# Evictions and pair combinations of the seven-product half-steps placed by scheduler priority

## The chip, the cores and the metric

One core of one Trainium2 chip runs the whole program. TensorE (PE in the rows; its weight loads are listed apart as PEld) multiplies, VectorE (DVE) and ScalarE (ACT) do arithmetic on tiles, GpSimd (POOL) and SyncE (SP) mainly issue transfers here. The metric is device time in microseconds for one execution, the median of several runs.

## The reference

The kernel is one inference step of a two-layer decoder: 512 tokens of a prompt and 8 sample tokens, 520 columns together, share all weights. Each layer is a half-step, a mixer (attention with a gated linear recurrence in layer 0, a matrix-memory recurrence in layer 1) and a second half-step. Only the four half-steps are touched by the change:

```python
D_MODEL = 1024; D_FF = 2816

def swiglu(x, w_gate, w_up, w_down):
    return (jax.nn.silu(x @ w_gate) * (x @ w_up)) @ w_down

def macaron_half(x, g, w_gate, w_up, w_down):
    return x + (0.5 * swiglu(rmsnorm(x, g), w_gate, w_up, w_down)).astype(x.dtype)

for li in range(DEPTH):          # DEPTH = 2
    x = macaron_half(x, g[0], ...)
    x = x + mixer(li, rmsnorm(x, g[1]))
    x = macaron_half(x, g[2], ...)
```

All arithmetic is in f32.

## The kernel before

**Numbers.** PE multiplies operands that are split into a high and a low part (`split`, L110 to L112: ACT casts the high part, `whi` for weights, then DVE subtracts it to make the low part, `wlo`). `dense` (L94 to L108) issues three matmuls for each 128x128 block: high by high, high by low, low by high (L106, L107, L108).

**A half-step** (`half_step`, called four times by `ffn`, at about 0, 785, 1145 and 1836 us of the span) goes over the 22 blocks of 128 hidden columns in groups of 6, 6, 6 and 4. The first four blocks, the lead gates, are plain products (`early`, tiles `g` and `u`); they run while the normalised input is still being made ready. After them come units: a `Gate` unit makes the hidden tile `h` of one block for all columns, a `Down` unit adds one pair of 128-row blocks to `x`. After every group but the last, eight `Down` units for that group stand between the first gate of the next group and the rest of them.

**A unit** is a two-by-two block product made with seven products instead of eight, named p1, q5, q6, p2, p3, p7 and p4 (`WHERE` tells which weights and which operand each takes). A product is 12 matmuls in a Gate unit or a Down unit of four blocks, 9 in a Down unit of three. Its three accumulators are PSUM banks: `A` takes p1, q6, p7 and p4, `B` takes p2, `E` takes q5 and p3. The products add up in a bank, which is why a bank is read between two products:

- after p1, ACT copies A to B (`evict`, L655);
- Gate: q5 is copied to `c5` by ACT (the rows' c<-E, L655), q6 to `h` by ACT, p2 goes through Silu on ACT (L519), p3 is added on DVE (L521) and goes through Silu on ACT, p7 is added to `c5` on DVE (c<-A, L524) and multiplied into `h` (L525), p4 is multiplied into `h` on DVE (L528);
- Down: each product is added to `x` on DVE (x<-A, x<-E, x<-B, L552).

The six banks go round in one pool. The loop over the units (`for f in seq`) issues, for each, `weights(f)`, p1 and q5, then p4 of the unit before, then q6, p2, p3 and p7. A matmul that goes on in a bank has to wait until that bank's last product was read.

**Weights.** `weights(f)` loads `graw` and `u2` on SP's queue, `raw` partly on SP's and, with an add on the way, on POOL's; then it makes five operands from them with three casts on ACT, three subtractions and two adds on DVE, and one more cast and subtraction for the sums. There are five buffers for full-size parts, two for `graw`; the pair tile of the lead gates shares one of the `graw` buffers.

**Pairs.** Two neighbouring Gate units fill one pair tile `h`. When both are done, `Pair.combine` makes the seven operands of the Down units: DVE instructions `cmb` (L468, L471, L472), casts `hh` on ACT and subtractions `hl` on DVE. It was called at the end of the odd gate's p4 and, for the lead pairs, once after the first unit's q5.

**What sets the order.** A scheduler places the instructions of all engines. Among those that could run it takes the one with the earliest place in the program; `tc.high_priority(n)` counts what is issued in its block as n places earlier. Weights' parts of a unit stand under `AHF` = 200. Evictions and combinations stood at their own place.

Of the kernel before, what the change touches and what calls it, by code (L numbers as in the profile page):

```python
# [35 lines left out]
REST = 4  # L36

AHM, AHF, AHE = 1, 200, 100
WHL = 5
SLOPE = [2.0 ** (-2 * (h + 1)) for h in range(4)]  # L40

# [20 lines left out]
class Net:  # L62
# [186 lines left out]
    def ffn(self, steps):  # L249
# [3 lines left out]
        with ExitStack() as ctx:  # L253
            self.wgrp = UNIT
            xp = self.pool(ctx, "ffnx")
            self.whl = self.pool(ctx, "whl", WHL)
            hp = self.pool(ctx, "ffn")
# [7 lines left out]
    def half_step(self, pos, first, last, xp, hp, pa):  # L265
# [9 lines left out]
        nc, tc = self.nc, self.tc  # L275
# [108 lines left out]
        def step():  # L384
            if steps and next(steps[0], 0) == 0:
                steps.pop(0)
# [54 lines left out]
        def bank(name):  # L441
            return pa.tile([P, 512], F32, tag="acc", name=name)

        def small():
            return hp.tile([P, n1], F32, tag="c5", name="c5")

        class Pair:
# [15 lines left out]
                self_split(hidden[0][:, self.i, j:j + b - a], hidden[1][:, self.i, j:j + b - a], self.h[:, a:b])  # L463

            def combine(self):
                x11, x22, x21, x12 = [self.h[:, i] for i in range(4)]
                cm = hp.tile([P, 4 * n1], F32, tag="cmb", name="cmb").rearrange("p (s t) -> p s t", s=4)
                nc.vector.tensor_tensor(out=cm[:, 0:2], in0=self.h[:, 0:2], op=ALU.subtract,  # L468
                                        in1=x12[:, None, :].to_broadcast([P, 2, n1]))
                self.parts(0, 3, 0)  # L470
                nc.vector.scalar_tensor_tensor(cm[:, 2], cm[:, 1], -1.0, x11, ALU.mult, ALU.subtract)  # L471
                nc.vector.scalar_tensor_tensor(cm[:, 3], cm[:, 2], -1.0, x21, ALU.mult, ALU.subtract)  # L472
                for a in (0, 2):
                    self_split(hidden[0][:, self.i, 3 + a:5 + a], hidden[1][:, self.i, 3 + a:5 + a], cm[:, a:a + 2])
# [6 lines left out]
        class Unit:  # L481

            def product(f, kind):
                w, v = WHERE[kind]
                n = n0 if kind in ("p1", "p2", "p4") else n1
                if kind == "p1":
                    f.A, f.B = bank("A"), bank("B")
                elif kind == "q5":
                    f.E = bank("E")
                ps = f.B if kind == "p2" else f.E if kind in ("q5", "p3") else f.A  # L490
                self.dense(ps[:, :n], f.w[w], lambda k: tuple(q[:, :n] for q in f.rhs(v, k)), ends=(kind in ("p1", "q5"), True),
                           open_=True)
                if kind == "p1":
                    self.evict(f.B[:, :n0], ps[:, :n0])
                f.out(kind, ps[:, :n])
                step()

        class Gate(Unit):
            nk = H
# [10 lines left out]
            def out(f, kind, ps):  # L510
                if kind in ("q6", "p2"):
                    f.pair.open()
                if kind == "q5":
                    f.c5 = small()
                    self.evict(f.c5, ps)
                elif kind == "q6":
                    self.evict(f.h(1), ps)
                elif kind == "p2":
                    nc.scalar.activation(f.h(0), ps, AF.Silu)  # L519
                elif kind == "p3":  # L520
                    nc.vector.tensor_tensor(out=f.h(1), in0=ps, in1=f.h(1), op=ALU.add)  # L521
                    nc.scalar.activation(f.h(1), f.h(1), AF.Silu)
                elif kind == "p7":
                    nc.vector.tensor_tensor(out=f.c5, in0=ps, in1=f.c5, op=ALU.add)  # L524
                    nc.vector.tensor_tensor(out=f.h(1), in0=f.h(1), in1=f.c5, op=ALU.mult)  # L525
                    f.done(1)
                elif kind == "p4":
                    nc.vector.tensor_tensor(out=f.h(0), in0=ps, in1=f.h(0), op=ALU.mult)  # L528
                    f.done(0)
                    if f.odd and not f.pair.plain:  # L530
                        f.pair.combine()

            def done(f, c):
                if f.pair.plain and not f.late:
# [1399 lines left out]
```

## Time and profile before

| | us |
|---|---|
| median of 3 runs | 2192.76 |
| lowest, highest run | 2188.43, 2197.22 |
| the profiled execution: time | 2194.01 |
| the profiled execution: span from the first to the last instruction | 2192.2 |
| PE busy in the span | 2130.5 |
| DVE busy | 1629.2 |
| ACT busy | 1108.1 |
| mean granted clock of PE (full speed is 1) | 0.992 |

The 1.8 us between time and span lie before the first and after the last instruction. Each row of a timeline is a start, a duration and, in brackets, the idle time of the engine before it with what ended it. Matmuls are pipelined: each lasts about 0.28 us, but the next starts 0.12 us later, so lost time on PE shows in the distance of starts.

### The profile page before, as it was taken

How to read it: one execution, taken by the hardware profiler on the slowest of the kernel's cores; microseconds unless marked ns; L12 is line 12 of the kernel's file. 1: busy time of each engine (PE TensorE's matmuls, PEld its weight loads, DVE VectorE, ACT ScalarE, POOL GpSimd, SP SyncE). 2: the span in 40 equal slices, each digit the busy share in tenths (PEclk: the TensorE clock that was granted, in tenths of full speed). 3: DMA queues.
4: the chain of work that ended last, by engine and by line, in shares of the span. 5: the costliest groups of instructions: out<-in, count | busy, mean ns of one | idle time of the engine just before them, and what ended most of it. 6: DMA issues, size and time to landing. Idle time of an engine off the chain costs nothing.

```text
span 2192.2 us, 46399 instructions
## 1 busy us (share of the span) xinstructions
PE 2130.5 (97%) x17908; PEld 2001.1 (91%) x17908; DVE 1629.2 (74%) x3409; ACT 1108.1 (51%) x2080; POOL 194.6 (9%) x276
## 2 busy tenths in 40 slices
PE   8999999999999999999999999999999999999999
PEld 8899999776776799999999999998989899999999
DVE  8888887434486587888877888877745588788884
ACT  6555555334523354556554565654555456455653
POOL 1011101000000001111100111100000000111110
PEclk9999999999999999999999999999999999999999
DMA  7487764478787745867733677653554564676872
GB/s 214 118 207 169 180 169 144 155 261 264 233 264 249 240 143 128 209 159 191 186 126 84 167 179 193 161 147 94 149 158 147 167 195 152 139 204 166 191 182 73
DMA packets 175763, 381.29 MB, mean 174 GB/s; under 512 B 16353, under 2 KB 51730, under 8 KB 175414
## 3 DMA queue, kind: packets, MB, share of 16 engines
q1 hardware_dynamic: 129600, 283.23, 39.6%
q0 software_dynamic: 40176, 82.05, 20.9%
q10 hardware_dynamic: 5766, 13.05, 1.6%
q8 instruction: 140, 2.29, 0.4%
q14 instruction: 81, 0.66, 0.1%
HBM read 361.15 MB, written 17.11 MB: 173 GB/s over the span
## 4 chain that ended last, share of the span: by engine, by line
PE 74%; DVE 13%; DMA 9%; ACT 3%; issue 2%; SPq 0%; ACTq 0%; DVEq 0%; POOLq 0%
PE A L106 9%; PE A L108 8%; PE A L107 8%; PE E L106 4%; PE E L107 4%; PE E L108 4%; DVE wlo L112 4%; PE pj L106 4%; PE pj L108 3%; PE pj L107 3%; PE y L106 2%; DMA raw<-w 2%; PE y L107 2%; PE y L108 2%; PE B L108 2%; PE B L107 2%
## 5 line engine op out<-in xcount | busy, mean ns | idle before, releaser
L112 DVE TENSOR_TENSOR wlo<-raw,whi 128x512 fp32r<-128x512 f32 (+2 forms) x344 | 311.9, 910 | 106.1 <-ACT whi L111 101.6
L111 ACT CAST whi<-raw 128x512 fp32r<-128x512 f32 (+2 forms) x344 | 273.2, 799 | 153.8 <-PE pj L107 76.6
L112 DVE TENSOR_TENSOR wlo<-graw,whi 128x1024 fp32r<-128x1024 f32 (+1 forms) x240 | 266.4, 1115 | 113.3 <-ACT whi L111 112.2
L111 ACT CAST whi<-graw 128x1024 fp32r<-128x1024 f32 (+1 forms) x240 | 231.2, 965 | 154.4 <-PE B L107 90.0
L106 PE MATMUL pj<-xh,whi 128*128 128x264 f32 (+1 forms) x896 | 258.8, 291 | 4.3 <-ACT kT L655 1.5
L106 PE MATMUL A<-xb,whi 128*128 128x264 f32 (+1 forms) x864 | 250.8, 290 | 8.2 <-DVE c L524 4.7
L108 PE MATMUL pj<-xh,wlo 128*128 128x264 f32 (+1 forms) x896 | 254.3, 285 | 1.5 <-DVE wlo L112 1.5
L107 PE MATMUL pj<-xl,whi 128*128 128x264 f32 (+1 forms) x896 | 255.0, 285 | 0.8 <-DVE xl L112 0.7
L107 PE MATMUL A<-xb,whi 128*128 128x264 f32 (+1 forms) x864 | 244.7, 283 | 0.6 <-DVE xb L112 0.6
L108 PE MATMUL A<-xb,wlo 128*128 128x264 f32 (+1 forms) x864 | 245.0, 284 | 0.0
L429 POOL DMA_DIRECT2D raw<-w x120 | 142.1, 1184 | 1141.3 <-DMA raw<-w 402.7
L106 PEld LDWEIGHTS pj<-xh,whi 128*128 128x128 f32 x896 | 169.1, 189 | 20.5 <-issue 9.5
L106 PEld LDWEIGHTS A<-xb,whi 128*128 128x128 f32 x864 | 163.4, 189 | 13.4 <-DVE c L524 5.9
L107 PEld LDWEIGHTS pj<-xl,whi 128*128 128x128 f32 x896 | 169.6, 189 | 5.1 <-DVE xl L112 2.5
L108 PEld LDWEIGHTS pj<-xh,wlo 128*128 128x128 f32 x896 | 169.6, 189 | 4.5 <-issue 2.7
L106 PE MATMUL A<-hh,whi 128*128 128x264 f32 (+1 forms) x576 | 165.5, 287 | 2.0
L106 PE MATMUL E<-xh,whi 128*128 128x264 f32 x576 | 163.6, 284 | 3.9 <-ACT c L655 3.9
L107 PEld LDWEIGHTS A<-xb,whi 128*128 128x128 f32 x864 | 163.1, 189 | 0.8 <-DVE xb L112 0.8
L107 PE MATMUL E<-xl,whi 128*128 128x264 f32 x576 | 163.4, 284 | 0.0
L108 PEld LDWEIGHTS A<-xb,wlo 128*128 128x128 f32 x864 | 163.3, 189 | 0.0
L108 PE MATMUL E<-xh,wlo 128*128 128x264 f32 x576 | 163.2, 283 | 0.0
L107 PE MATMUL A<-hl,whi 128*128 128x264 f32 (+1 forms) x576 | 162.7, 282 | 0.0
(491 smaller groups left out, 6266.9 us busy)
## 6 DMA issues: line engine op xcount, KB each, us to landing
raw<-w SPq DMA_DIRECT2D x168, 512.0 KB, 4.2
raw<-w POOLq DMA_DIRECT2D x112, 512.0 KB, 6.9
graw<-w SPq DMA_DIRECT2D x72, 512.0 KB, 4.2
kt<-ckt SPq DMA_DIRECT2D x128, 256.0 KB, 4.4
vtile<-cv SPq DMA_DIRECT2D x128, 256.0 KB, 4.0
u<-w SPq DMA_DIRECT2D x72, 256.0 KB, 3.7
raw<-w SPq DMA_DIRECT2D x48, 384.0 KB, 3.7
raw<-w POOLq DMA_DIRECT2D x48, 384.0 KB, 5.6
```

The source lines that it names most:

```text
L106: nc.tensor.matmul(ps, lhsT=wh, rhs=xh, start=(ends[0] and i == ks[0]), stop=False, skip_group_check=open_)
L107: nc.tensor.matmul(ps, lhsT=wh, rhs=xl, start=False, stop=False, skip_group_check=open_)
L108: nc.tensor.matmul(ps, lhsT=wl, rhs=xh, start=False, stop=(ends[1] and i == ks[-1]), skip_group_check=open_)
L111: self.nc.scalar.copy(out=hi, in_=src)
L112: self.nc.vector.tensor_tensor(out=lo, in0=src, in1=hi, op=ALU.subtract)
L429: nc.gpsimd.dma_start(out=s2, in_=w[f.u0:f.u0 + 2, :, :B].rearrange("u p c -> p u c"), accum_op=ALU.add)
```

## The change

A product's `out` (the evictions after q5, q6, p2, p3, p7 and p4, and what is computed from them) is issued under a priority of 300 places, so ahead of the weights' parts of a later unit, which stand at 200. The copy of A to B after p1 stays as it was. A pair's combination is issued under a priority of 100 places, in a new method `after` that is called once `out` is done; the lead pairs' combination takes the same path. Nothing is added to or removed from any engine's instructions.

```diff
 AHM, AHF, AHE = 1, 200, 100
+AHO, AHC = 300, 100
 
             def combine(self):
+                with tc.high_priority(AHC):
+                    self.combined()
+
+            def combined(self):
                 x11, x22, x21, x12 = [self.h[:, i] for i in range(4)]
...
                 if kind == "p1":
                     self.evict(f.B[:, :n0], ps[:, :n0])
-                f.out(kind, ps[:, :n])
+                with tc.high_priority(AHO):
+                    f.out(kind, ps[:, :n])
+                f.after(kind)
                 step()
+
+            def after(f, kind):
+                pass
...
                     f.done(0)
-                    if f.odd and not f.pair.plain:
-                        f.pair.combine()
+
+            def after(f, kind):
+                if kind == "p4" and f.odd and not f.pair.plain:
+                    f.pair.combine()
```

Lines move by one near the top of the file and by ten to twelve lower down: L106 becomes L107, L112 becomes L113, L524 becomes L534, L552 becomes L564, L655 becomes L667.

DVE at the first hand-over from Down units to the next Gate unit (first half-step). A_2550 and A_2648 are the A banks of the last two Down units of the group, E_2660 the last one's E; 2721 to 2733 are the weights of the Gate unit behind them. Before:

```order
L552 SCALAR_TENSOR_TENSOR x_69<-E_2562,x_69 128x264
L112 TENSOR_TENSOR wlo_2729<-graw_2721,whi_2728 128x1024
L112 TENSOR_TENSOR wlo_2737<-raw_2725,whi_2736 128x1024
L432 TENSOR_TENSOR graw_2721<-graw_2721,raw_2725 128x512
L552 SCALAR_TENSOR_TENSOR x_69<-A_2550,x_69 128x264
L432 TENSOR_TENSOR graw_2721<-graw_2721 128x512
L552 SCALAR_TENSOR_TENSOR x_69<-E_2660,x_69 128x264
L552 SCALAR_TENSOR_TENSOR x_69<-A_2648,x_69 128x264
L552 SCALAR_TENSOR_TENSOR x_69<-A_2550,x_69 128x256
L112 TENSOR_TENSOR wlo_2733<-u2_2723,whi_2732 128x512
```

After:

```order
L564 SCALAR_TENSOR_TENSOR x_69<-E_2562,x_69 128x264
L113 TENSOR_TENSOR wlo_2729<-graw_2721,whi_2728 128x1024
L564 SCALAR_TENSOR_TENSOR x_69<-A_2550,x_69 128x264
L113 TENSOR_TENSOR wlo_2737<-raw_2725,whi_2736 128x1024
L564 SCALAR_TENSOR_TENSOR x_69<-E_2660,x_69 128x264
L433 TENSOR_TENSOR graw_2721<-graw_2721,raw_2725 128x512
L564 SCALAR_TENSOR_TENSOR x_69<-A_2550,x_69 128x256
L113 TENSOR_TENSOR wlo_2733<-u2_2723,whi_2732 128x512
L564 SCALAR_TENSOR_TENSOR x_69<-A_2648,x_69 128x264
L433 TENSOR_TENSOR graw_2721<-graw_2721 128x512
```

The evictions of the two Down units now stand between the parts of the next unit's weights: the one of A_2550 behind one subtraction, where it stood behind two and an add.

ACT at the start of the second half-step. A_13094, B_13095 and E_13109 are the banks of the second Gate unit there, 13191 to 13195 the weights of the third. Before:

```order
L655 ACTIVATE B_13095<-A_13094 128x256
L111 CAST whi_13198<-graw_13191 128x1024
L111 CAST whi_13206<-raw_13195 128x1024
L111 CAST whi_13202<-u2_13193 128x512
L655 ACTIVATE c5_13122<-E_13109 128x264
L655 ACTIVATE h_13025<-A_13094 128x264
L519 ACTIVATE h_13025<-B_13095 128x256
```

After:

```order
L667 ACTIVATE B_13095<-A_13094 128x256
L112 CAST whi_13198<-graw_13191 128x1024
L667 ACTIVATE c5_13122<-E_13109 128x264
L112 CAST whi_13206<-raw_13195 128x1024
L112 CAST whi_13202<-u2_13193 128x512
L667 ACTIVATE h_13025<-A_13094 128x264
L529 ACTIVATE h_13025<-B_13095 128x256
```

The copy of E to c5 stood behind three casts of the next unit's weights and now stands behind the first.

DVE at the same place, some 7 us on; A_13094 again, 13325 to 13329 are the weights of the fourth unit. Before:

```order
L112 TENSOR_TENSOR wlo_13213<-graw_13191,whi_13212 128x1024
L112 TENSOR_TENSOR wlo_13333<-graw_13325,whi_13332 128x768
L112 TENSOR_TENSOR wlo_13341<-raw_13329,whi_13340 128x768
L432 TENSOR_TENSOR graw_13325<-graw_13325,raw_13329 128x384
L524 TENSOR_TENSOR c5_13122<-A_13094,c5_13122 128x264
L432 TENSOR_TENSOR graw_13325<-graw_13325 128x384
```

After:

```order
L113 TENSOR_TENSOR wlo_13213<-graw_13191,whi_13212 128x1024
L534 TENSOR_TENSOR c5_13122<-A_13094,c5_13122 128x264
L113 TENSOR_TENSOR wlo_13333<-graw_13325,whi_13332 128x768
L535 TENSOR_TENSOR h_13025<-h_13025,c5_13122 128x264
L113 TENSOR_TENSOR wlo_13341<-raw_13329,whi_13340 128x768
L433 TENSOR_TENSOR graw_13325<-graw_13325,raw_13329 128x384
```

The eviction c5<-A_13094 (of p7) moved up over two subtractions and an add.

PE at the same start. A_12955 is the A bank of the first Gate unit, whose p4 is due. Before:

```order
L106 MATMUL A_13094<-xh_70,whi_13076 128x256
L107 MATMUL A_13094<-xl_71,whi_13076 128x256
L108 MATMUL A_13094<-xh_70,wlo_13077 128x256
L106 MATMUL E_13109<-xh_70,whi_13084 128x264
L107 MATMUL E_13109<-xl_71,whi_13084 128x264
L108 MATMUL E_13109<-xh_70,wlo_13085 128x264
```

After:

```order
L107 MATMUL A_13094<-xh_70,whi_13076 128x256
L108 MATMUL A_13094<-xl_71,whi_13076 128x256
L109 MATMUL A_13094<-xh_70,wlo_13077 128x256
L107 MATMUL A_12955<-xb_12394,whi_12941 128x256
L107 MATMUL E_13109<-xh_70,whi_13084 128x264
L108 MATMUL E_13109<-xl_71,whi_13084 128x264
```

The first matmul of the first unit's p4 now stands between p1 and q5 of the second; its other eleven stand behind q5 as before. One unit on, the first matmul of A_13094's p4 moved in the same way.

At the start of the first half-step the three cmb instructions of the first lead pair moved up DVE's order by some 13 to 15 places, to between the lead gates' own evictions (h<-g).

## Rows read from the trace of the kernel before

**Rows 1.** The page's first part: busy us, share of the span, instructions.

```profile
PE 2130.5 (97%) x17908; PEld 2001.1 (91%) x17908; DVE 1629.2 (74%) x3409; ACT 1108.1 (51%) x2080; POOL 194.6 (9%) x276
```

**Rows 2.** Waits of PE by releaser: us in total, times, longest.

```profile
PE A L106 <- DVE c L524: 4.7, 5, 1.4
PE E L106 <- ACT c L655: 3.9, 4, 1.1
```

**Rows 3.** The same view of the weight loads.

```profile
PEld A L106 <- DVE x L552: 7.1, 24, 0.4
```

**Rows 4.** Stretches: length, busy us (instructions) by engine, granted clock, DMA share, GB/s.

```profile
160.00:200.00 40.00, 40.00 (x333) 39.79 (x331) 34.33 (x60) 22.62 (x39) 4.96 (x6) 1.00 0.69 152
840.00:880.00 40.00, 37.70 (x308) 36.99 (x307) 33.38 (x53) 22.11 (x38) 3.75 (x5) 1.00 0.59 134
```

**Rows 5.** Timeline of PE, first hand-over: start, us, line, operation, idle before.

```profile
214.47 0.28 PE L108 MATMUL A<-hh,wlo 128*128 128x264 f32 x1
214.78 0.39 PE L106 MATMUL A<-hh,whi 128*128 128x256 f32 x1
```

**Rows 6.** Timeline of DVE, the same hand-over.

```profile
211.42 1.23 DVE L112 TENSOR_TENSOR wlo<-graw,whi 128x1024 fp32r<-128x1024 f32 x1
212.56 1.22 DVE L112 TENSOR_TENSOR wlo<-raw,whi 128x1024 fp32r<-128x1024 f32 x1
...
214.30 0.42 DVE L552 SCALAR_TENSOR_TENSOR x<-A,x 128x264 f32<-128x264 f32 x1
```

**Rows 7.** Timeline of PE, start of the second half-step.

```profile
852.30 0.28 PE L106 MATMUL E<-xh,whi 128*128 128x264 f32 x1
...
858.24 0.28 PE L108 MATMUL B<-xh,wlo 128*128 128x256 f32 x1
859.43 0.39 PE L106 MATMUL E<-xh,whi 128*128 128x264 f32 x1 [0.91 <-ACT c L655]
...
863.86 0.28 PE L106 MATMUL E<-xh,whi 128*128 128x264 f32 x1
...
867.10 0.39 PE L106 MATMUL A<-xb,whi 128*128 128x256 f32 x1 [1.36 <-DVE c L524]
```

**Rows 8.** Timeline of ACT, the same start.

```profile
856.57 1.05 ACT L111 CAST whi<-graw 128x1024 fp32r<-128x1024 f32 x1 [2.91 <-DMA graw<-w]
...
859.00 0.38 ACT L655 ACTIVATE c<-E 128x264 f32<-128x264 f32 x1
```

**Rows 9.** Timeline of DVE, the same start.

```profile
853.46 0.42 DVE L524 TENSOR_TENSOR c<-A,c 128x264 f32<-128x264 f32 x1
...
863.27 2.10 DVE L112 TENSOR_TENSOR wlo<-graw,whi 128x1024 fp32r<-128x1024 f32 x2 [0.78 <-ACT whi L111]
865.28 0.95 DVE L112 TENSOR_TENSOR wlo<-raw,whi 128x768 fp32r<-128x768 f32 x1
...
866.62 0.43 DVE L524 TENSOR_TENSOR c<-A,c 128x264 f32<-128x264 f32 x1
```

**Rows 10.** Timeline of PE: the longest idles of the first and before the third half-step.

```profile
76.52 0.59 PE L106 MATMUL A<-xb,whi 128*128 128x264 f32 x1 [3.55 <-ACT h L655]
...
1148.87 0.58 PE L106 MATMUL g<-xh,whi 128*128 128x256 f32 x1 [2.61 <-ACT xh L111]
```

**Rows 11.** Timeline of ACT, start of the first half-step.

```profile
72.86 1.04 ACT L111 CAST whi<-graw 128x1024 fp32r<-128x1024 f32 x1 [2.42 <-DMA graw<-w]
...
76.08 0.38 ACT L655 ACTIVATE h<-A 128x264 f32<-128x264 f32 x1
```

**Rows 12.** Stretches behind those two idles, columns as in rows 4.

```profile
77.00:80.00 3.00, 3.00 (x16) 3.00 (x16) 3.00 (x6) 0.95 (x3) 0.00 (x0) 0.54 0.18 54
...
1149.00:1158.00 9.00, 9.00 (x43) 9.00 (x44) 7.41 (x26) 2.61 (x7) 0.00 (x0) 0.50 0.17 56
```

**Rows 13.** Timeline of DVE, combination of the first pair.

```profile
69.06 0.70 DVE L468 TENSOR_TENSOR cmb<-h 128x528 f32<-128x528 f32 x1
...
70.58 0.43 DVE L471 SCALAR_TENSOR_TENSOR cmb<-cmb,h 128x264 f32<-128x264 f32 x1
```

## Prediction

> **What bounds the kernel now.** I read the page's busy shares first. TensorE (PE) is busy 97% of the span, DVE 74% and ACT 51% [rows 1]. So DVE and ACT as totals limit nothing, and a change of order can only pay where PE stands still or runs at the lower clock.
>
> Second I read PE's waits by releaser. Those that the change can touch are few: 4.7 us for the eviction c<-A on DVE (L524) and 3.9 us for c<-E on ACT (L655) [rows 2]. The longest single idle lies in the first half-step and is told in part 3. The same view for the weight loads adds what the matmul rows hide because it is short: 24 waits, 7.1 us in all, for x<-A of the down products, none over 0.4 us [rows 3].
>
> Third, a table by stretches says where they sit. A steady stretch has PE busy 40.00 of 40 us. The start of the second half-step has not, 37.70 [rows 4]; the third and fourth read like it, and the first is worse. So there are two places: the starts, where the first seven-product units meet late weights, and the three hand-overs per half-step from the last down unit to the next gate unit, where the short waits lie.
>
> **Part 1: the hand-overs.** In the first, PE starts a matmul at 214.47 and the next, p4 of the last down unit but one, at 214.78 [rows 5]. A steady stretch sets them 40/333 = 0.12 apart [rows 4], so 0.19 is lost, and the start after that follows 0.22 later, which loses 0.10 more. That is 0.3 us, and a hand-over has two such waits: 0.6 us. Twelve hand-overs make 7.4 us, near the 7.1 of the weight loads' row.
>
> The wait ends with x<-A, which starts at 214.30 and takes 0.42. Its bank was full at about 211.3 (27 matmuls of 0.12 us before 214.6), but it stood on DVE behind two casts and an add, from 211.42 [rows 6]. The order now has it behind the first cast only, so it would start at 212.56 and end at 213.0. PE now wants it earlier too, since p4 stands ahead of q6: nine matmuls, 1.1 us, before 214.6, so at 213.5. The margin is 0.5 us. At the second place, the p4 behind the next gate's p1, the order lifts x<-A over two casts and two adds, more than the twelve matmuls by which PE comes sooner. **I take 6.5 of the 7.4 us**, since the last hand-over of each half-step has the combine's casts on DVE beside it; bounds 0 (each wait only moves to the next bank) and 7.4.
>
> By the Trainium skill, "Perfetto Trace Analysis", section Optimization Strategy, the same gap repeating on the engine that should be saturated can mean that there isn't enough SBUF or PSUM for the next tile. By that rule the 24 waits would stay, since no buffer is added, and part 1 would be 0. The rows speak for the order of DVE instead: the bank was full three microseconds before its eviction began.
>
> **Part 2: starts of half-steps 2 to 4.** Two idles each. The first, 0.91 us at 859.43, is p3 waiting for bank E, freed by c<-E on ACT at 859.00 [rows 7]. That eviction stood behind three casts, which began at 856.57 when the weights landed [rows 8]. With the order of after it stands behind one: 856.57 + 1.05 + 0.38 gives 858.0, before PE wants the bank, 0.12 after 858.24. The wait goes: 1.19 − 0.12 for the start and 0.10 for the slow second matmul, so 1.2 us.
>
> The second, 1.36 us at 867.10, is the next p4 behind c<-A on DVE at 866.62 [rows 7, 9]. With the added starts the loss is about 1.7 us. The eviction stood behind two wlo<-graw, one wlo<-raw and an add; now it stands behind one wlo<-graw. It would start at 863.27 + 1.14 = 864.4 and end at 864.8, 2.2 us earlier. But PE comes for it earlier too: p4's first matmul now stands ahead of q5's twelve, right behind p1. PE was at that place at 863.86 [rows 7], and will now be at 863.3 (1.2 us earlier by the first wait, 0.6 later by the next point). So it waits 1.5, and 0.9 if the weights land 0.65 earlier: graw now takes the slot of the lead pair's tile, and the combine that frees it has its last step ahead of a wlo<-graw instead of behind it; 0.65 is what walking DVE's order from 848 us on gives, an estimate. I take 1.3.
>
> New is a wait at the p4 before: its first matmul too stands ahead of q5, so PE wants c<-A at 852.30 [rows 7], and not after q5. It ended at 853.89 [rows 9]; DVE's order now puts it ahead of two hl casts of 0.6 us, at about 852.85. So 0.55 us, with 0.10 of restart 0.65. Queued behind a waiting matmul is all of PE; DVE's and ACT's next casts wait for the weights, not for PE, so nobody else pays.
>
> Sum for one start: 1.2 + 1.7 before; 0.65 + 0 + 1.3 after. **Gain about 1.0 each, three starts 3.0 us.** Bounds: −0.5 each (no earlier landing, and the first p4 waits until 853.9 as before) to 2.9 each (both go). I stay near the middle because the second p4 hangs on the landing of graw, which no row of before shows for the new slot.
>
> **Part 3: the start of the first half-step.** PE idles 3.55 us at 76.52 for h<-A, which ACT ran at 76.08 behind whi<-graw, whi<-raw and a cast that waited for cmb on DVE [rows 10, 11]. Now h<-A stands behind whi<-graw alone: 72.86 + 1.04, so 73.9 and 2.2 us sooner, if graw lands as before. After the idle the granted clock is 0.54 over 77 to 80 us [rows 12], 16 matmuls where 25 would fit, 1.1 us lost. A shorter idle should spare that: the idle of 1.36 at 867.10 left the clock at 1.00 in the row of its stretch [rows 4]. Gain up to 2.2 + 1.1 = 3.3.
>
> Against it stands that the first pair's combine is now ahead of the lead gates' evictions h<-g on DVE: 0.70 + 0.43 + 0.43 us [rows 13], so evictions of lead banks are up to 1.5 us later. **I take a gain of 2.0**, 3.3 less most of that 1.5; bounds −1.5 (the pushed evictions cost in full and the idle of 3.55 stays because graw lands later) and 5.7 (the 3.55, the 1.1 of clock and the 1.1 that is the longest wait of E for c [rows 2] all go).
>
> Everything else that moves (gate evictions behind casts in the steady stretches, hh and hl casts, a few SP and POOL places) I cost at nothing: PE is busy 40.00 of 40 us there, with six banks, so a shift of under a microsecond is under its slack. If that cover is gone it shows as PE waits in the steady stretches, 0.1 to 0.4 us each.
>
> **The sum.** 6.5 + 3.0 + 2.0 = 11.5 us off the profiled 2194.0, which is 2182.5; off the median, 1.2 us lower than the profiled run, 2181.3. **Forecast 2181.5**, on the scale of the median. A measurement tells about 0.5%, 11 us, from no change: the bound is 2181.8, so the likeliest case sits on it.
>
> **The rivals.** *A: the waits move.* The evictions win their places and what they displace, the casts of the next weights, comes late by as much: a hand-over's p1 then waits for wlo, as PE did for graw at the starts. For: DVE works 34.33 of 40 us in such a stretch [rows 4], so slack is short. Against: each cast is displaced by one or two evictions of about 0.35, while a unit has 84 matmuls, 10 us, or 63, 7.6 us, to make it up. Half of part 1, nothing of part 2, 2.0 of part 3: 5.3 us, 2187.5. By the skill's rule above (waits of the hand-overs unchanged) parts 2 and 3 alone give 5.0: 2187.8, the same place; I give it a tenth of the chance of this case.
>
> *B: slower.* The p4 set ahead of q5 makes PE wait in one piece where it waited in two. Before, an idle of 3.55 us ended at the lower clock, 0.54, and one of 2.61 us at 1148.87 was followed by 0.50 over 1149 to 1158 [rows 10, 12], 43 matmuls where 75 would fit, 3.8 us lost; 1.36 was free. If graw lands no earlier and c<-A falls behind a second cast, the second p4 waits 1.5 + 1.14 = 2.6 us: past the idle that cost 3.8. Then each of three starts costs 0.65 at the first p4 and 2.6 + 3.8 at the second against 2.9 before: 4.1 us lost, 12.4 in all, with parts 1 and 3 at half (4.3) a net +8.1: 2200.9. It decides at a wait between 1.4 and 2.6 us. Against: two casts must stand ahead, and the order shows one.
>
> *C: nothing happens.* PE is busy 97%; if the waits are merely where the weights' pace is absorbed, the whole is within 3 us: 2190.
>
> *D: more.* All three parts near their upper bounds, 7.4 + 6 + 4 = 17.4 off the median: 2175.4.
>
> **How the numbers follow.** Forecast's case 0.50 (2178 to 2185, a little over half of it, 0.29, beyond the bound, as its centre is), A 0.19, B 0.10, C 0.05, D 0.16. Faster by over 0.5%: D and that part of the forecast's case, 0.16 + 0.29 = 0.45. Slower by over 0.5%: B, 0.10. Within it: the rest, 0.45. The range leaves out B and the far end of D: 2174.5 to 2193.
>
> **What would show it.** Part 1: the 24 waits for x<-A in the weight loads' rows fall to a few. Part 2: no wait of E for c in half-steps 2 to 4, one of about 0.5 and one of about 1.3 for c<-A, clock 1.00 in these stretches. Part 3: the idle at 76.52 under 2 us and the clock behind it near 1.00. Wrong would be: new waits for wlo in the hand-overs (A), a clock near 0.5 behind the starts (B), steady stretches under 39.8 of 40.

## The result and the profile after

The changed kernel takes 2181.22 us in the median of 8 runs (2174.64 to 2188.95), the kernel before 2193.32 in 8 runs beside it (2188.43 to 2197.22): a ratio of 0.9948, 95% interval 0.9928 to 0.9968. The forecast was 2181.5. Measured again beside the experiments, the ratio was 0.9958 (0.9942 to 0.9973).

The profiled execution of after took 2174.64 us with a span of 2172.9, the lowest of its 8 runs; so its 19.4 us under the profile of before are more than the change is worth, and the stretches have to be told apart. The stretch from the first to the last seven-product matmul of each half-step is 285.6, 280.7, 281.0 and 280.8 us before, and 282.4, 276.7, 277.5 and 277.5 after: 14.2 us less in all (12.6 in a second profile of the same kernel, below). The rest of the 19.4 is mostly the plain lead products of the second and third half-step, 5.7 us shorter, which the change does not touch; why that of the third (4.1 of the 5.7) differs is told at the end.

The first part of the page of after (busy us, share, instructions) shows the same work:

```profile
PE 2119.0 (98%) x17908; PEld 1994.4 (92%) x17908; DVE 1626.1 (75%) x3409; ACT 1111.5 (51%) x2080; POOL 194.7 (9%) x276
```

PE's waits by releaser in after, the rows that answer to [rows 2]:

```profile
PE A L107 <- DVE c L534: 5.6, 5, 1.8
PE A L107 <- ACT h L667: 2.6, 1, 2.6
...
PE A L107 <- ACT B L667: 0.9, 1, 0.9
```

The wait of E for c<-E is gone; the one for c<-A is longer than before. In the view of the weight loads the row of [rows 3], x<-A with 24 waits, is gone. From 120 to 365 us, where the first half-step has its three hand-overs and before had six of the 24, one is left:

```profile
PEld A L107 <- DVE x L564: 0.2, 1, 0.2
```

DVE at the first hand-over in after, against [rows 6]:

```profile
209.32 1.23 DVE L113 TENSOR_TENSOR wlo<-graw,whi 128x1024 fp32r<-128x1024 f32 x1
210.46 0.43 DVE L564 SCALAR_TENSOR_TENSOR x<-A,x 128x264 f32<-128x264 f32 x1
210.80 1.22 DVE L113 TENSOR_TENSOR wlo<-raw,whi 128x1024 fp32r<-128x1024 f32 x1
```

The eviction follows the first subtraction, 1.14 us after that began; before, 2.88 us passed (211.42 to 214.30).

The start of the second half-step. Two rows by stretches, each 45 us from the first seven-product matmul, of before and of after; a full one has 375 matmuls:

```profile
842.19:887.19 45.00, 42.70 (x350) 41.99 (x349) 38.85 (x65) 23.44 (x41) 4.94 (x6) 1.00 0.57 136
```

```profile
836.65:881.65 45.00, 43.65 (x363) 43.45 (x362) 38.63 (x66) 23.91 (x41) 4.94 (x6) 1.00 0.57 141
```

PE, ACT and DVE there in after, against [rows 7], [rows 8] and [rows 9]:

```profile
846.75 0.28 PE L107 MATMUL A<-xb,whi 128*128 128x256 f32 x1
...
856.72 0.28 PE L109 MATMUL A<-xh,wlo 128*128 128x256 f32 x1
858.35 0.39 PE L107 MATMUL A<-xb,whi 128*128 128x256 f32 x1 [1.35 <-DVE c L534]
```

```profile
849.90 1.05 ACT L112 CAST whi<-graw 128x1024 fp32r<-128x1024 f32 x1 [2.52 <-DMA graw<-w]
850.86 0.39 ACT L667 ACTIVATE c<-E 128x264 f32<-128x264 f32 x1
```

```profile
855.53 0.42 DVE L531 TENSOR_TENSOR h<-E,h 128x264 f32<-128x264 f32 x1
856.73 1.23 DVE L113 TENSOR_TENSOR wlo<-graw,whi 128x1024 fp32r<-128x1024 f32 x1 [0.77 <-ACT whi L112]
857.87 0.43 DVE L534 TENSOR_TENSOR c<-A,c 128x264 f32<-128x264 f32 x1
```

The first p4 (846.75) goes through without a wait, c<-E stands right behind the first cast, and one wait is left: p4 of the second unit, for c<-A behind a wlo<-graw for which DVE itself had waited 0.77 us.

In what follows, **lost time** is what successive starts on PE stand apart beyond 0.1205 us (264 columns) or 0.1185 us (256 columns), summed where it is over 0.05; a **start** is the first 45 us of a seven-product stretch (60 us in the first half-step), the **rest** is what comes after, and there the hand-overs are. In before the starts lose 8.2, 3.2, 3.6 and 3.4 us and the rests 3.5 each. In after the starts lose 6.8, 1.6, 2.4 and 2.4, the rests 1.8, 1.3, 1.3 and 1.3.

### The profile page after: what moved, and what is told of

It is laid out like the page before. It is cut to its first block, busy times and chain, and to the rows that moved or that the text cites. A ratio compares the mean times of both kernels' runs of the same rounds, so it can differ in the third digit from the quotient of the medians.

```text
span 2172.9 us, 46406 instructions
## 1 busy us (share of the span) xinstructions
PE 2119.0 (98%) x17908; PEld 1994.4 (92%) x17908; DVE 1626.1 (75%) x3409; ACT 1111.5 (51%) x2080; POOL 194.7 (9%) x276
## 5 line engine op out<-in xcount | busy, mean ns | idle before, releaser
L113 DVE TENSOR_TENSOR wlo<-raw,whi 128x512 fp32r<-128x512 f32 (+2 forms) x344 | 312.1, 911 | 103.8 <-ACT whi L112 99.1
L113 DVE TENSOR_TENSOR wlo<-graw,whi 128x1024 fp32r<-128x1024 f32 (+1 forms) x240 | 267.6, 1115 | 127.8 <-ACT whi L112 127.3
L112 ACT CAST whi<-raw 128x512 fp32r<-128x512 f32 (+2 forms) x344 | 273.2, 799 | 143.5 <-PE pj L108 77.4
L112 ACT CAST whi<-graw 128x1024 fp32r<-128x1024 f32 (+1 forms) x240 | 230.1, 964 | 172.6 <-PE B L108 101.4
L107 PE MATMUL pj<-xh,whi 128*128 128x264 f32 (+1 forms) x896 | 259.4, 291 | 5.1 <-ACT whi L112 1.4
L107 PE MATMUL A<-xb,whi 128*128 128x264 f32 (+1 forms) x864 | 249.2, 288 | 9.3 <-DVE c L534 5.6
L107 PEld LDWEIGHTS pj<-xh,whi 128*128 128x128 f32 x896 | 169.5, 190 | 21.2 <-issue 9.5
L107 PEld LDWEIGHTS A<-xb,whi 128*128 128x128 f32 x864 | 162.9, 189 | 14.2 <-DVE c L534 7.3
L107 PE MATMUL E<-xh,whi 128*128 128x264 f32 x576 | 163.3, 283 | 0.0
L107 PE MATMUL A<-hh,whi 128*128 128x256 f32 (+1 forms) x576 | 163.1, 283 | 0.0
L108 PE MATMUL A<-hl,whi 128*128 128x256 f32 (+1 forms) x576 | 162.7, 282 | 0.3 <-DVE hl L113 0.3
```

What stands on the lines that cost most here:

```text
L107: nc.tensor.matmul(ps, lhsT=wh, rhs=xh, start=(ends[0] and i == ks[0]), stop=False, skip_group_check=open_)
L108: nc.tensor.matmul(ps, lhsT=wh, rhs=xl, start=False, stop=False, skip_group_check=open_)
L112: self.nc.scalar.copy(out=hi, in_=src)
L113: self.nc.vector.tensor_tensor(out=lo, in0=src, in1=hi, op=ALU.subtract)
```

## Experiments

**One part alone.** Three runs take the change apart. The first prioritises only the Down units' evictions:

```diff
-                with tc.high_priority(AHO):
-                    f.out(kind, ps[:, :n])
+                if isinstance(f, Down):
+                    with tc.high_priority(AHO):
+                        f.out(kind, ps[:, :n])
+                else:
+                    f.out(kind, ps[:, :n])
...
-                with tc.high_priority(AHC):
-                    self.combined()
+                self.combined()
```

> Only the Down units' evictions go ahead; Gate evictions and combinations stand as before. My theory (each wait is an eviction standing behind the next weights' casts on its engine, so the hand-overs are the Down units' own matter): the 24 weight-load waits for x<-A fall from 7.1 us to under 1, PE's waits in the starts stay (c<-E about 3.9 us, c<-A about 4.7, h<-A 3.5), the stretch from the first to the last seven-product matmul of half-steps 2 to 4 is 278.4 to 278.8 us each where before has 280.7 to 281.0, and the time is 8 us under before, 0.996. Rival of the buffers (the same gap repeats because a bank or tile is not free): the 24 waits stay and the time is that of before, 1.000.

Measured: 0.9968 (0.9953 to 0.9982), 2184.61 us. No wait for x<-A is left, the rests lose 1.5 us each instead of 3.5, and the starts still lose 7.7, 3.1, 4.5 and 3.8, so that two of the three stretches came out longer than expected (279.9 and 279.1 us). PE's waits:

```profile
PE A L107 <- DVE c L536: 6.2, 6, 1.4
PE E L107 <- ACT c L669: 4.9, 4, 2.0
```

So the hand-overs are the matter of the Down units' evictions alone, and they are some two thirds of the gain.

The second does the same for the Gate units (`isinstance(f, Gate)`), without the combinations.

> Only the Gate units' evictions go ahead. My theory: the 24 waits for x<-A stay at about 7 us; the wait of E for c<-E goes from the starts of half-steps 2 to 4 and one longer wait for c<-A of 1.3 to 1.8 us is left in each; those stretches are 279 to 279.8 us, and the time 4 to 5 us under before, 0.998. Rival (the two groups of evictions only work together, as one DVE queue serves both): the starts gain under 1 us in all and the time is that of before.

Measured: 0.9999 (0.9980 to 1.0018). The hand-overs wait as before:

```profile
PEld A L107 <- DVE x L566: 7.2, 25, 0.4
```

The wait for c<-E is gone, as expected. The gain of 4 to 5 us is not there: the starts lose 9.2, 5.4, 4.2 and 2.4 us. This expectation failed; in half-steps 2 and 3 the third unit's weights landed 1.1 and 0.7 us later than in before (table below).

The third leaves `f.out` without a priority and keeps that of the combinations.

> Only the pairs' combinations go ahead (100 places). My theory: the 24 waits for x<-A and the waits of the starts stay within 0.5 us each, weights of the third unit land a few tenths of a microsecond earlier, time 0.999 to 1.001. Rival (the combination, which frees the tile into which the third unit's weights land, is what shortened the starts): the stretches of half-steps 2 to 4 are 1 us shorter each and nothing is left of the wait for c<-E.

Measured: 1.0012 (0.9995 to 1.0029). Starts lose 7.3, 3.0, 3.8 and 4.0, rests 3.5 to 4.0. The third unit's weights did not land sooner, against the expectation (table below). By itself this part gains nothing.

**More banks.** The kernel before with another split of PSUM:

```diff
-            pa = self.pool(ctx, "pacc", 6, space=PSUM)
-            pst = self.pool(ctx, "pst", 2, space=PSUM)
+            pa = self.pool(ctx, "pacc", 7, space=PSUM)
+            pst = self.pool(ctx, "pst", 1, space=PSUM)
```

> The kernel before with seven PSUM banks for the accumulators instead of six (one instead of two for the statistics). My theory: the waits for x<-A are for one named bank whose own next product is due, so a further bank changes nothing: 24 waits, 7 us, time 0.999 to 1.003. Rival of the buffers: the 24 waits fall below half and the time is 3 to 7 us lower.

Measured: 1.0028 (1.0006 to 1.0050). The weight loads' row reads as in [rows 3]:

```profile
PEld A L106 <- DVE x L552: 7.1, 24, 0.4
```

A seventh bank takes none of the 24 waits away. The run has one bank less for the statistics too; whether the start of the first half-step, which lost 11.9 us instead of 8.2, has to do with that was not tested.

**What sets a start's loss.** The starts varied between runs of like order, so I set each loss beside the moment of the first ACT cast that waits for the third unit's graw (the **landing**), counted from the first seven-product matmul, for half-steps 2, 3 and 4 of five profiles:

| kernel | cast at, us | lost, us | difference |
|---|---|---|---|
| before | 14.38, 14.79, 14.55 | 3.21, 3.62, 3.39 | 11.17, 11.17, 11.16 |
| Down only | 14.32, 15.69, 14.94 | 3.14, 4.52, 3.78 | 11.18, 11.17, 11.16 |
| Gate only | 15.52, 15.47, 13.70 | 5.40, 4.16, 2.42 | 10.12, 11.31, 11.28 |
| combinations only | 14.26, 15.11, 15.31 | 2.98, 3.80, 4.02 | 11.28, 11.31, 11.29 |
| the change | 13.25, 14.07, 14.06 | 1.61, 2.42, 2.41 | 11.64, 11.65, 11.65 |

The loss is the landing less a constant of the order. The one exception, the 10.12, is a start in which the clock fell behind the wait (below), which costs 1.2 us more. The next run tells whether the combinations' priority counts beside the evictions'. Its edit is the last two lines of the first diff (`self.combined()` without a priority).

> All evictions go ahead (300 places), the combinations stand as before. In the runs so far the time lost in a start of half-steps 2 to 4 is the moment at which ACT casts the third unit's graw, counted from the first seven-product matmul, less a constant: less 11.17 us in the order of before (14.38 us and 3.21 lost; 15.69 and 4.52), less 11.64 in the order of the change (13.25 and 1.61). My theory now: evictions' order gives the constant, the combination's place gives an earlier landing; so here landing at 14.4 or later, losses of 2.8 to 3.5 in each start, hand-overs clean as in the changed kernel, time 0.996. Rival: the combination's priority does nothing even beside the evictions', landing 13.3 to 14.1 and the time of the changed kernel, 0.9948.

Measured: 0.9983 (0.9967 to 0.9999), 2187.14 us, so above the times of both expectations and slower than the change. Casts at 14.96, 14.90 and 14.59, lost 3.66, 3.59 and 4.38; rests 1.3 to 1.8. The landing is as late as I expected, but the difference is 11.30 and 11.31 in the first two and not 11.64: the order of the evictions does not give the change's constant by itself. In half-step 4 the wait was 2.16 us and the clock fell behind it. In half-step 3 of the same execution a wait of the same 2.16 us had no such effect; the rows of PE and the stretches show both, half-step 3 first:

```profile
1213.51 0.39 PE L107 MATMUL A<-xb,whi 128*128 128x256 f32 x1 [2.16 <-DVE c L533]
...
1894.50 0.39 PE L107 MATMUL A<-xb,whi 128*128 128x256 f32 x1 [2.16 <-DVE c L533]
```

```profile
1213.51:1216.51 3.00, 3.00 (x25) 3.00 (x26) 3.00 (x5) 0.78 (x3) 1.18 (x1) 1.00 0.59 140
1894.50:1897.50 3.00, 3.00 (x16) 3.00 (x17) 3.00 (x5) 0.74 (x3) 1.17 (x1) 0.63 0.40 140
```

The clock also fell in the Gate-only run (half-step 2, a wait of 2.16 us, 5.4 lost). That is rival B's mechanism. In the change the same wait was 1.35 to 1.75 us in the six starts of its two profiles, and no fall followed; that the sooner landing keeps it clear of one is likely and not shown.

**The order of products.** In after, c<-A at 857.87 had a full bank while DVE idled. This run lets p7 go ahead of p3:

```diff
-            for kind in ("q6", "p2", "p3", "p7"):
+            for kind in ("q6", "p2", "p7", "p3"):
...
                     nc.scalar.activation(f.h(1), f.h(1), AF.Silu)
+                    nc.vector.tensor_tensor(out=f.h(1), in0=f.h(1), in1=f.c5, op=ALU.mult)
+                    f.done(1)
                 elif kind == "p7":
                     nc.vector.tensor_tensor(out=f.c5, in0=ps, in1=f.c5, op=ALU.add)
-                    nc.vector.tensor_tensor(out=f.h(1), in0=f.h(1), in1=f.c5, op=ALU.mult)
-                    f.done(1)
```

> The changed kernel with p7 ahead of p3 in every unit, so that the eviction c<-A has two products' time before p4 wants its bank (the multiplication into h moves to p3's eviction). In the profile of the changed kernel DVE idles 0.77 us at 856.73 and then works off wlo<-graw ahead of c<-A, whose bank was full: my theory is that the wait of 1.3 to 1.9 us is only this place in the queue, so it goes to under 0.3 in half-steps 2 to 4, 4 to 5 us in all, and the time is 0.992 to 0.9935. Rival: the start is bound by the landing of graw itself, the wait turns up at the next product that needs those weights (q6 of the third unit, for wlo) and the time is that of the changed kernel, 0.9948.

Measured: 0.9984 (0.9971 to 0.9998), slower than both expectations. c<-A is no longer waited for in the starts of half-steps 2 to 4, but h<-A is, everywhere:

```profile
PEld A L107 <- ACT h L667: 17.7, 32, 2.6
```

p7 now follows q6 in bank A with one product between them, and ACT has not copied q6 out by then. The starts lose 1.9, 3.1 and 3.0 with casts at 13.32, 14.47 and 14.39: there the wait changed its name and stayed (the difference is 11.4). The loss against the change lies in the rests, 2.2, 2.2, 2.2 and 2.8 where the change has 1.3 to 1.8. My theory that only the place of c<-A cost was wrong.

The same edit on the kernel before:

> The kernel before with p7 ahead of p3 and nothing else. My theory: it takes away waits of p4 behind c<-A in the starts but not the hand-overs, whose x<-A stand behind casts either way (the p7 eviction gains one product's time, 1.1 us, and stands 2 us behind): 10 or more of the 24 waits stay, time 0.997 to 1.000. Rival (product order alone is the cure): the 24 waits go and the time equals that of the changed kernel or less, 0.993 to 0.995.

Measured: 1.0017 (1.0000 to 1.0034). No wait for x<-A is left, which I had not expected, but others stand in their place, so the rival's time did not come either. The weight loads' rows:

```profile
PEld A L106 <- ACT h L655: 20.4, 34, 3.8
PEld A L106 <- DVE c L526: 6.5, 19, 0.8
```

**The change again**, for a second profile.

> The changed kernel once more, for a second profile. My theory: the hand-overs and the constant of 11.64 us repeat within 0.1 us, the three stretches of half-steps 2 to 4 lie within 276.5 to 278; what differs from profile to profile is the lead (47.8 to 53 us, by the clock behind its first idle), the landing and the mixers. Rival: the gain in the starts was one profile's luck, landing 14.4 to 15.5 and 3 to 4 us lost in each.

Measured: 0.9958 (0.9942 to 0.9973). Casts at 13.35, 14.42 and 14.17, lost 1.69, 2.77 and 2.52: differences of 11.66, 11.65 and 11.65. Rests 1.5, 1.3, 1.3 and 1.3. The first half-step's start lost 7.9, so its gain is 1.4 us in one profile and 0.3 in the other.

**The landing taken away.** In the changed kernel the third unit's graw waits for the tile of the second lead pair: it is issued at 844.84, when the last cmb, which reads that tile, has ended.

```profile
844.34 0.43 DVE L477 SCALAR_TENSOR_TENSOR cmb<-cmb,h 128x264 f32<-128x264 f32 x1
...
844.84 0.34 SPq L424 DMA_DIRECT2D graw<-w  x1
```

(In before it took the other buffer, at 851.65, when the second unit's last wlo<-graw had ended at 851.63; the pair's tile was not free until 851.97.) A second `stg` tile frees it of that, but needs 4 KB per partition, which the kernel's other tiles do not leave; with four buffers for the weights' parts they do. The first run is the changed kernel with `WHL = 4` alone, the second has both edits:

```diff
-WHL = 5
+WHL = 4
...
-                                     bufs=2 if tag == "graw" else None).rearrange("p (s t) -> p s t", s=4)
+                                     bufs=2).rearrange("p (s t) -> p s t", s=4)
...
-                f.pair.open("stg" if i < 2 else "graw")
+                f.pair.open("stg")
```

> The changed kernel with four instead of five buffers for the weights' parts: a control for the run beside it, which needs the room. Expected by either theory: weights' casts start later, the time is 1 to 3% over the changed kernel or the same; only the starts are compared.

> The control with a second tile for lead pairs, so that the third unit's graw no longer waits for the second lead pair's combination. My theory (a start's loss is that landing and the chain of casts behind it): graw of the third unit is issued and cast several microseconds earlier than in the control, the loss of 2 to 3 us in the starts of half-steps 2 to 4 falls under 1, and the wait for h<-A of 2.3 to 2.6 us in the first half-step falls too; 6 to 8 us under the control in the four seven-product stretches. Rival (the places of the evictions in ACT's and DVE's queues set the loss): the same waits for c<-A as in the control, within 0.5 us each.

Measured: the control 0.9938 (0.9918 to 0.9958), 2179.73 us; with its own slot 0.9872 (0.9837 to 0.9908), 2166.31 us in 4 runs (2162.54 to 2167.68). The control did not get slower, against my expectation, and its starts were a little shorter already (4.2, 1.2, 2.2 and 0.9), its rests longer (1.9 to 2.0). With the slot the third unit's graw is issued 0.5 us before the first seven-product matmul of half-step 2 and not 8.4 us behind it, and its cast, at 9.8 us instead of 11.9, waits for no transfer. The starts lose 2.5, 0.3, 0.3 and 0.3, the rests 1.2 each. The four seven-product stretches sum to 1103.3 us, against 1111.5 in the control and 1113.9 in after: 8.2 of the 13.4 us between the two medians. Where the other 5 come from was not followed up. The 45 us from the first seven-product matmul of half-step 2, control and then own slot:

```profile
834.05:879.05 45.00, 44.42 (x367) 44.00 (x366) 39.68 (x66) 24.81 (x42) 4.92 (x6) 1.00 0.58 143
```

```profile
831.34:876.34 45.00, 45.00 (x375) 44.86 (x374) 40.65 (x68) 25.92 (x43) 5.04 (x7) 1.00 0.57 134
```

All that is left, with the slot, of PE's waits for evictions in the seven-product units:

```profile
PE A L107 <- ACT h L667: 0.5, 1, 0.5
PE E L107 <- ACT c L667: 0.4, 1, 0.4
PE A L107 <- ACT B L667: 0.2, 1, 0.2
```

**The slot without the change**: the last edit on the kernel before.

> The kernel before (no priorities for evictions or combinations) with the second tile for lead pairs and four buffers for parts, as in e10. If the starts were bound by the third unit's landing alone, their loss goes here as it did in e10 (from 3.2 to 3.6 us to under 0.7 in half-steps 2 to 4), while the Down units' evictions still stand in their old places, so that hand-overs keep several microseconds of waits for x<-A: about 9 to 14 us over e10, 0.992 to 0.995. If the evictions' places matter in the starts too, 1 to 3 us are still lost in each for c<-A or c<-E, and the time is 0.995 to 1.000. If the slot alone is the cure for everything, the time is that of e10, 0.987.

Measured: 0.9932 (0.9911 to 0.9953), 2179.25 us, 13 us over the run with both. Half of the waits of the hand-overs are left, and each start of half-steps 2 to 4 loses 1.1 us, most of it in one wait for c<-A:

```profile
PEld A L106 <- DVE x L552: 4.1, 12, 0.6
```

```profile
850.04 0.39 PE L106 MATMUL A<-xb,whi 128*128 128x256 f32 x1 [0.76 <-DVE c L524]
```

So in the starts the landing is the larger part (3.4 us lost on average before, 1.1 here) and the evictions' places are the rest (0.3 with the change). How much of what this run gains, in the starts and in the hand-overs, comes from the slot and how much from having four buffers for parts was not told apart in the old order.

**The combinations further ahead**: `AHO, AHC = 300, 150`.

> The changed kernel with the combinations 150 places ahead instead of 100. The order puts the first unit's c<-A ahead of the second unit's last wlo<-graw and the lead pair's hl casts ahead of an add; the step of the combination that frees the tile stands 0.6 us sooner. My theory: landing 0 to 0.6 us sooner after the first seven-product matmul, starts 0 to 0.6 us shorter each, time within 2 us of the changed kernel (0.994 to 0.996). Rival (the combination's priority by itself takes room from weights' parts): starts longer, 0.996 to 0.998.

Measured: 0.9931 (0.9904 to 0.9958), 2176.06 us in 6 runs, whose interval overlaps that of the change. Casts at 13.46, 14.19 and 14.63, lost 1.81, 2.55 and 2.98 (differences of 11.64 to 11.65), so nothing is gained in half-steps 2 to 4. The start of the first lost 3.9 instead of 6.8 and 7.9, in one profile.

## Why the prediction was right

**Part 1, the hand-overs,** was right in its mechanism and too small. It was to bring 6.5 us; the rests lost 14.2 us before and 5.6 in each profile of after, 8.5 less, more than the upper bound of 7.4. The mis-sized term is the 0.6 us of a hand-over, read from the first and multiplied by twelve: the third of each half-step loses 0.77 (0.32 and 0.25 with 0.10 behind each). The discount for the combination's casts was not needed either: the last hand-overs of half-steps 2 to 4 are as clean as the others. The Down-only run shows the part by itself. By the rule of the Trainium skill, "Perfetto Trace Analysis", section Optimization Strategy, a repeated gap can mean that PSUM ran out; the run with a seventh bank does not agree with it here, 24 waits and 7.1 us as before. The buffers were there, and the instruction that empties one stood too far back in its queue.

**Part 2, the starts of half-steps 2 to 4,** came out at 3.8 us in one profile and 3.2 in the other, for a forecast of 3.0. Its steps: the wait for c<-E did go. The wait at the first p4, put at 0.65, was 0, 0.40 and 0.58. It was not new: in before p4 stood behind q5 and still lost 0.30, 0.48 and 0.62 there, which my 2.9 for a start left out, as the idle column shows none of it in half-step 2:

```profile
853.62 0.28 PE L108 MATMUL E<-xh,wlo 128*128 128x264 f32 x1
853.94 0.38 PE L106 MATMUL A<-xb,whi 128*128 128x256 f32 x1
```

The second p4 was to lose 1.3 and lost 1.6, 2.0 and 1.8. What was wrong is the picture of separate waits, each with its own price. The loss of a start is one quantity, the landing of the third unit's weights less a constant. The 1.2 us of the wait for c<-E were therefore not saved as such; of the 1.2 us that a start gained (3.41 lost on average before, 2.24 in six starts of after), 0.48 is the change of the constant, from 11.17 to 11.65, and 0.7 the sooner landing, on average from 14.57 to 13.89. That landing I had put at 0.65, walking DVE's order, and had counted only in part. It needs both priorities, and so does the constant: evictions alone landed at 14.8 on average and had 11.3.

**Part 3, the first half-step,** was put at 2.0 and is 1.4 in one profile and 0.3 in the other. The step that failed is "if graw lands as before": the cast of [rows 11] at 72.86, 13.89 us from the first seven-product matmul, came at 14.65 and 14.36 instead, so the idle ended 1.5 and 1.8 us sooner than before and not 2.2. Its length fell from 3.55 to only 2.57 and 2.28 us, not to 1.35, because PE also came to it 0.5 us sooner (13.5 instead of 14.0 us from the first seven-product matmul), which costs nothing by itself. The 1.1 us of the clock were saved in the first profile and not in the second, where it fell again (last section). The waits for B, wlo and hl, 0.3 to 0.9 us each in after, are new.

**The sum** was 11.5; the three parts as measured give 13.7 us (8.5, 3.8 and 1.4) and 12.0 (8.5, 3.2 and 0.3), the median moved by 12.1, and its interval allows 7 to 16. That the forecast came within 0.3 us of the median is luck: part 1 was 2.0 us too small, part 3 up to 1.7 too large, and the interval is wider than either.

**The rivals.** *A* (the casts come late instead): no wait for wlo appeared in the hand-overs. *B* (slower through the clock) did not happen in the change, but its mechanism is real: in three starts without the combinations' priority the wait at the second p4 reached 2.16 us, and behind two of them the clock fell. Its price of 3.8 us for such an idle was too high: in those two the fall cost 1.1 and 1.2 us (11.3 less 10.2 and 10.1), in the third nothing. *D* (more) was reached, and passed, by the run with the slot, for a reason that the rival did not name.

## What to carry over

Where a saturated engine has short waits that repeat, look at where the releasing instruction stands in its engine's queue before adding buffers: moving the Down units' evictions ahead of casts that are not due took 8 us here, and no other wait grew in the hand-overs. A wait that changes its name when the order is changed (c<-E, c<-A, h<-A) has a common cause further up; plotting the loss against the arrival of the data showed it in one table, and taking away what held the transfer back removed it. A change whose parts do nothing alone can still need them together: the combinations' priority counts only with the evictions'.

## What the runs showed of the hardware

The clock behind an idle is not told by the idle's length. PE before the third half-step idles 2.61 us in both profiles. In before, 0.50, the lower of its two levels (1.2 GHz), was granted for the next 9 us and 43 matmuls ran [rows 10, 12]. In after:

```profile
1139.32 0.39 PE L107 MATMUL g<-xh,whi 128*128 128x256 f32 x1 [2.61 <-ACT xh L112]
```

```profile
1139.32:1148.32 9.00, 9.00 (x75) 8.90 (x76) 8.74 (x32) 3.14 (x8) 0.00 (x0) 1.00 0.18 58
```

75 matmuls in the same 9 us at full clock (2.4 GHz): 4 us of the profile's difference, from the same instructions. The first half-step agrees: behind 2.57 us of idle after kept 1.00, and its second profile, behind only 2.28, fell to 0.65, a mean over a stretch that has both levels:

```profile
74.90:77.90 3.00, 2.98 (x25) 2.98 (x26) 2.88 (x6) 2.23 (x6) 0.00 (x0) 1.00 0.00 0
```

```profile
74.70:77.70 3.00, 3.00 (x17) 3.00 (x18) 2.33 (x5) 1.77 (x4) 0.00 (x0) 0.65 0.00 0
```

The waits of 2.16 us in the evictions-only run, one followed by 1.00 and one by 0.63, are a third case, within one execution. What decides it was not settled. It is one source of the differences between two profiles of one kernel, so single profiles are to be compared stretch by stretch, and a price for an idle of 2 to 3 us should be given as a range that begins at nothing.
